# RMSNorm with GELU on one core: the first group scaled and stored row by row, its stores in 8 KB pieces

## The chip, the core and the metric

The kernel runs on one core of a Trainium2 chip. Times are device microseconds (us) of that core, taken from whole executions; the span in a profile is about 1.8 us shorter than the time of the same execution. Engines are named as in the profile: ACT (ScalarE), DVE (VectorE), POOL (GpSimd), PE (TensorE), SP (SyncE, which here only issues loads). "Faster" or "slower" needs a difference of 2%.

## The reference, cut

```python
# x: (8, 1024, 2048) float32, gamma: (2048,)
rms = np.sqrt(np.mean(x ** 2, axis=-1, keepdims=True) + eps)
out = gamma * x / rms
return 0.5 * out * (1 + np.tanh(np.sqrt(2 / np.pi) * (out + 0.044715 * out ** 3)))
```

Each of the 8192 rows is read once and written once: 67.1 MB in and 67.1 MB out.

## The kernel before

The rows are cut into 16 groups. A group has 128 partitions with 4 consecutive rows each, so a partition's share is 32 KB of contiguous memory, and a group is 4 MB. There are six slots in on-chip memory. A group is loaded whole, squared and summed row by row on ACT, scaled by gamma on DVE in place, put through GELU on ACT in place (with 1/rms as the scale of the activation), and stored whole from ACT's queue. The slot is then free for the load of group g + 6.

```python
P, ROWS, SLOTS = 128, 4, 6
x3 = ... .rearrange("(g p r) d -> g p r d", p=P, r=R)      # cut
slot = [sbuf.tile([P, R, D], FP32, name=f"slot{i}") for i in range(SLOTS)]

store_pieces = {G - 1: [(0, 2), (2, 2)]}
scale_pieces = {G - 1: [(0, 1), (1, 1), (2, 1), (3, 1)]}

def load(g):
    nc.sync.dma_start(out=slot[g % SLOTS], in_=x3[g])

def squares(g):                       # 4 ACT activations with accum_out (cut)
def scale(g):
    for r, n in scale_pieces.get(g, [(0, R)]):
        ...                           # one DVE multiply by gamma of n rows (cut)

def gelu_store(g):
    for r, n in store_pieces.get(g, [(0, R)]):
        for q in range(r, r + n):
            row = slot[g % SLOTS][:, q, :]
            nc.scalar.activation(out=row, in_=row, func=ACT.Gelu_apprx_tanh,
                                 scale=rstd[:, g, q : q + 1])
        nc.scalar.dma_start(out=o3[g, :, r : r + n, :],
                            in_=slot[g % SLOTS][:, r : r + n, :])

for g in range(SLOTS):
    load(g)
...                                   # gamma, constants (cut)
for g in range(G + 1):
    if g < G:
        squares(g); inverse_rms(g); scale(g)
    if g:
        gelu_store(g - 1)
        if g - 1 + SLOTS < G:
            load(g - 1 + SLOTS)
```

## Time and profile before

| | before |
|---|---|
| time, median of 3 | 317.33 us (317.2 to 317.46) |
| ACT busy | 79% |
| DVE busy | 44% |
| moved by DMA | 134.25 MB at 424 GB/s |
| a 32 KB packet on one DMA engine | 1.213 us (432 GB/s over 16 engines) |
| first store issued | 38.6 us |
| load 6, the first that needs a free slot, issued | 64.0 us |

The page of the kernel before, of a profiled execution that took 318.66 us and is not one of the three timed. The "DMA" row gives the busy share of the 16 DMA engines in 40 equal slices of the span, in tenths; the row under it is what they moved. The line with percent signs is the chain of waits that ended last, as shares of the span. The last two lines are the transfers, with KB each and the median us from issue to landing.

```profile
span 316.9 us, 473 instructions
...
PE 7.2 (2%) x8; PEld 2.5 (1%) x8; DVE 139.4 (44%) x21; ACT 251.1 (79%) x194; POOL 32.3 (10%) x101
...
DMA  8999999999999999999999999999999999999995
GB/s 328 414 451 426 434 393 459 401 459 402 459 405 455 426 434 431 430 434 426 438 426 455 410 455 418 443 426 430 434 430 435 422 459 405 459 414 447 422 420 230
DMA packets 4787, 134.25 MB, mean 424 GB/s; under 512 B 544, under 2 KB 560, under 8 KB 560
...
DMA 56%; ACT 33%; issue 5%; ACTq 1%; SPq 0%
...
slot<-in_x_dram SPq DMA_DIRECT2D x16, 4096.0 KB, 37.1
out_dram<-slot ACTq DMA_DIRECT2D x15, 4096.0 KB, 38.6
```

The DMA row is full from the second slice to the next to last.

The trace also holds every DMA packet with its start, duration, size and queue. "Packet time" is the sum of the durations of all load and store packets, divided by 16: what an average DMA engine had to do. "Stretch" is the time from the first packet's start to the last packet's end. For this profile the stretch is 313.83 us and the packet time 312.23 us: the engines worked almost without a break. At 1.213 us per 32 KB packet the bytes alone need about 310.5 us. By the profile's own zero of time the first packet starts at 1.7 us and the last ends at 315.6 us; the prediction below has both some 0.35 us later, and it rounds the rate to 433 GB/s and the time of the bytes to 309.7 us.

ACT has waits of its own. From the list of waits (total us, times, longest us):

```profile
...
ACT junk L65 <- DMA slot<-in_x_dram: 43.7, 11, 10.3
```

From the timeline of ACT (start us, us, instruction, and in brackets the idle time before it with its releaser), the place that the change works on:

```profile
...
30.93 7.67 ACT L101 ACTIVATE slot<-slot,rstd 128x2048 f32<-128x2048 f32 x4
...
38.62 0.36 ACTq L105 DMA_DIRECT2D out_dram<-slot  x1
```

From the timeline of SP's queue, the first load that has to wait for a free slot (with the one after it, merged in one line):

```profile
...
63.96 19.69 SPq L61 DMA_DIRECT2D slot<-in_x_dram  x2
```

And the end, from the timeline of ACT:

```profile
...
276.24 1.88 ACT L65 ACTIVATE junk<-slot 128x2048 f32<-128x2048 f32 x1 [3.66 <-DMA slot<-in_x_dram]
...
300.64 0.34 ACTq L105 DMA_DIRECT2D out_dram<-slot  x1
```

The GELU of group 0 begins at 30.9 us, because ACT squares group 1 first, and the whole group's store is issued at 38.6 us. The load at 63.96 us is load 6, which had to wait until that store had landed. At the end, the last load has landed by 276.2 us and the last store, 2.1 MB or some 5 us of DMA work, is issued at 300.6 us. By the packet records the DMA engines work until 315.6 us: even at the end ACT is ahead of them.

### The profile page before, as it was taken

The numbers are of one execution on the slowest core, as the hardware profiler recorded it, in microseconds if no ns is written. First come the engines' busy times: TensorE is split into PE (matmuls) and PEld (weight loads), VectorE is DVE, ScalarE is ACT, GpSimd is POOL, SyncE is SP. The second block draws the span as 40 slices with busy tenths as digits, with TensorE's granted clock in tenths as the row PEclk, the third lists the DMA queues.
The fourth block names the chain that finished last, engine by engine and source line by source line (L and its number), as shares of the span: only waits on it lengthen the run. The fifth ranks groups of instructions, "written<-read, shape, count | busy, mean of one in ns | idle before, by whom it ended". The sixth has DMA issues, their size and how long they took to land.

```text
span 316.9 us, 473 instructions
## 1 busy us (share of the span) xinstructions
PE 7.2 (2%) x8; PEld 2.5 (1%) x8; DVE 139.4 (44%) x21; ACT 251.1 (79%) x194; POOL 32.3 (10%) x101
## 2 busy tenths in 40 slices
PE   0900000000000000000000000000000000000000
PEld 0300000000000000000000000000000000000000
DVE  0038909090919191732808246091550905582000
ACT  1379999999999997959689595995959859599800
POOL 0020102020202020202002020020200102001000
DMA  8999999999999999999999999999999999999995
GB/s 328 414 451 426 434 393 459 401 459 402 459 405 455 426 434 431 430 434 426 438 426 455 410 455 418 443 426 430 434 430 435 422 459 405 459 414 447 422 420 230
DMA packets 4787, 134.25 MB, mean 424 GB/s; under 512 B 544, under 2 KB 560, under 8 KB 560
## 3 DMA queue, kind: packets, MB, share of 16 engines
q1 hardware_dynamic: 2304, 67.11, 49.5%
q10 hardware_dynamic: 2480, 67.12, 49.1%
q14 instruction: 3, 0.02, 0.0%
HBM read 67.12 MB, written 67.11 MB: 424 GB/s over the span
## 4 chain that ended last, share of the span: by engine, by line
DMA 56%; ACT 33%; issue 5%; ACTq 1%; SPq 0%
DMA slot<-in_x_dram 30%; DMA out_dram<-slot 26%; ACT slot L101 19%; ACT junk L65 14%; ACTq L105 1%; SPq L61 0%; ACTq L101 0%; ACTq L65 0%
## 5 line engine op out<-in xcount | busy, mean ns | idle before, releaser
L75 DVE TENSOR_TENSOR slot<-slot,gamma_ps 128x8192 f32<-128x8192 f32 (+1 forms) x19 | 139.2, 7340 | 147.0 <-ACT junk L65 147.0
L65 ACT ACTIVATE junk<-slot 128x2048 f32<-128x2048 f32 x64 | 120.4, 1881 | 47.3 <-DMA slot<-in_x_dram 43.7
L101 ACT ACTIVATE slot<-slot,rstd 128x2048 f32<-128x2048 f32 x64 | 122.8, 1989 | 0.9 <-ACT slot L101 0.9
L85 POOL TENSOR_SCALAR ms<-ssq 128x4 f32<-128x4 f32 x16 | 3.1, 194 | 247.5 <-ACT junk L65 247.5
L89 POOL TENSOR_TENSOR y<-ms,power 128x4 f32<-128x4 f32 x16 | 16.1, 1009 | 1.3
L65 ACT ACTIVATION_READ_ACCUMULATOR junk<-slot 128x1 f32 x64 | 12.0, 188 | 0.0
L121 PE MATMUL gamma_ps<-gamma_row,ones 1*128 1x512 f32 x8 | 7.2, 1072 | 8.4 <-DMA gamma_row<-in_gamma_dram 8.4
L95 POOL TENSOR_TENSOR rstd<-z,y 128x4 f32<-128x4 f32 x16 | 3.2, 201 | 1.3
L91 POOL TENSOR_TENSOR z<-z,ms 128x4 f32<-128x4 f32 x16 | 3.2, 201 | 1.3
L90 POOL TENSOR_TENSOR z<-y 128x4 f32<-128x4 f32 x16 | 3.2, 199 | 1.3
L92 POOL TENSOR_SCALAR z<-z 128x4 f32<-128x4 f32 x16 | 3.1, 194 | 1.4
L121 PEld LDWEIGHTS gamma_ps<-gamma_row,ones 1*128 1x128 f32 x8 | 2.5, 325 | 11.5 <-issue 11.5
L119 ACT ACT_TABLE_LOAD x1 | 1.3, 1283 | 1.3 <-PEq L153 1.3
L117 DVE MEMSET warm<- 1x1 f32 x1 | 0.1, 59 | 0.8 <-PEq L153 0.8
L119 ACT ACTIVATE warm<-warm 1x1 f32<-1x1 f32 x1 | 0.2, 202 | 0.0
L118 DVE MEMSET ones<- 1x128 f32 x1 | 0.2, 165 | 0.0
L116 POOL MEMSET power<- 128x4 f32 x1 | 0.1, 102 | 0.3 <-POOLq L153 0.3
L153 POOL MEMSET const-float32-0.0<- 128x1 f32 x1 | 0.1, 99 | 0.2 <-issue 0.2
L153 POOL MEMSET const-bfloat16-1.0<- 128x1 bf16 x1 | 0.1, 102 | 0.0
L153 POOL MEMSET const-uint8-127<- 128x1 uint8 x1 | 0.1, 102 | 0.0
L153 POOL MEMSET const-float32-1.0<- 128x1 f32 x1 | 0.1, 99 | 0.0
## 6 DMA issues: line engine op xcount, KB each, us to landing
slot<-in_x_dram SPq DMA_DIRECT2D x16, 4096.0 KB, 37.1
out_dram<-slot ACTq DMA_DIRECT2D x15, 4096.0 KB, 38.6
out_dram<-slot ACTq DMA_DIRECT2D x2, 2048.0 KB, 15.0
gamma_row<-in_gamma_dram ACTq DMA_DIRECT2D x1, 8.0 KB, 7.5
```

The source lines that it names most:

```text
L65: nc.scalar.activation(out=junk, in_=slot[g % SLOTS][:, r, :], func=ACT.Square, accum_out=ssq[:, g, r : r + 1],)
L75: nc.vector.tensor_tensor(out=rows, in0=rows, in1=gamma_ps.unsqueeze(1).to_broadcast([P, n, D]), op=ALU.mult,)
L85: v.tensor_scalar(out=ms, in0=ssq[:, g, :], scalar1=1.0 / D, scalar2=eps_f, op0=ALU.mult, op1=ALU.add,)
L89: v.tensor_tensor(out=y, in0=ms, in1=power, op=ALU.pow)
L90: v.tensor_tensor(out=z, in0=y, in1=y, op=ALU.mult)
L91: v.tensor_tensor(out=z, in0=z, in1=ms, op=ALU.mult)
L92: v.tensor_scalar(out=z, in0=z, scalar1=-0.5, scalar2=1.5, op0=ALU.mult, op1=ALU.add)
L95: v.tensor_tensor(out=rstd[:, g, :], in0=z, in1=y, op=ALU.mult)
L101: nc.scalar.activation(out=row, in_=row, func=ACT.Gelu_apprx_tanh, scale=rstd[:, g, q : q + 1],)
L105: nc.scalar.dma_start(out=o3[g, :, r : r + n, :], in_=slot[g % SLOTS][:, r : r + n, :])
L119: nc.scalar.activation(out=warm, in_=warm, func=ACT.Gelu_apprx_tanh)
L121: nc.tensor.matmul(out=gamma_ps[:, k : k + 512], lhsT=ones, rhs=gamma_row[:, k // GW : (k + 512) // GW, 0:GW], start=True, stop=True,)
```

## The change

The intent is to send the first output off earlier: once row 0 of group 0 has its GELU, it goes out, while rows 1 to 3 are still in work. DVE's multiply is cut by rows too.

```diff
-    store_pieces = {G - 1: [(0, 2), (2, 2)]}
-    scale_pieces = {G - 1: [(0, 1), (1, 1), (2, 1), (3, 1)]}
+    single = [(0, 1), (1, 1), (2, 1), (3, 1)]
+    store_pieces = {0: single, G - 1: [(0, 2), (2, 2)]}
+    scale_pieces = {0: single, G - 1: single}
```

A row of a partition is 8 KB, and the next partition's row is 32 KB further on, so a row's store consists of 128 pieces of 8 KB where the whole group's store had 128 pieces of 32 KB.

## The prediction

> **What bounds it now.** The DMA engines. The page shows 134.25 MB at a mean of 424 GB/s. In the transfer records the 16 engines hold packets without a gap from 2.1 us to 315.9 us of the 316.9 us span. A 32 KB packet takes 1.213 us on one engine (433 GB/s over 16), load or store; at that pace the bytes need 309.7 us. The rest the change hardly touches: 2.1 us before the first packet, 1.0 us after the last, 0.7 us of slow first load packets, 0.6 us of slow packets near 41 us, where the first store arrives, and small dips.
>
> ACT (79%) isn't the limit: the waits show 43.7 us for loads, from 119 us on about 3.7 us a group. DVE (44%) waits for ACT.
>
> **How the rings share.** From the first store on, each engine's records alternate load packet, store packet, both 32 KB. The Trainium skill, "DMA: Bandwidth & Descriptors", section "Queues, rings and completion order", says engines round-robin between queue rows by packet; this trace agrees, with one 32 KB descriptor acting as the packet. The first store was issued at 38.6 us and landed at 63.9 us; only then was load 6 issued.
>
> **What changes.**
> - DVE: one scale of 8.69 us becomes four of about 2.2 us, starting after the first square (15.2 us, not 21.3). ACT gains nothing: it squares group 1 until 31.0 us anyway.
> - ACT: 3 more store issues of 0.34 us, and broken GELU pipelining (7.67 us for four in a row, 3.90 for two): about +1.5 us where ACT is 96% busy. The first store goes out at about 33.2 us.
> - DMA: same bytes; 384 more data packets and 48 more completion writes (4787 become about 5219). From 16 KB at 0.611 us and 32 KB at 1.213 us I estimate 0.31 us for 8 KB, +0.2 us in all.
> - Sharing: an 8 KB store packet alternates with a 32 KB load packet, so the first stores get a fifth of the bandwidth while loads 4 and 5 are queued. An estimate, stepping the rings with these durations: load 5 lands near 68 us, not 82; load 6 is issued at 71 to 76 us, not 64. The load ring is then empty some 4 us, but the store ring holds rows of group 0 and all of group 1, so no engine idles. Later loads land earlier, stores queue longer; the last load lands some 8 us before its 276 us.
>
> **How much is critical.** Almost none. A change of order helps only where DMA idles, and only the fixed ends do. Ending ACT earlier (last store issued at 300.6 us, last packet at 315.9) only lengthens the store backlog.
>
> Prediction: 317.6 us, 316.9 to 318.6 in 8 of 10. Chances: faster by 2% 0.01, within 2% 0.97, slower 0.02.
>
> **What would show the steps.** Packets near 5219; 8 KB packets near 0.31 us; first stores issued at 33 to 41 us; load 6 issued past 70 us; no slice of low DMA share between 40 and 80 us; store landings longer and load landings shorter (medians now 38.6 and 37.1 us).
>
> **What would make it wrong.** Dearer 8 KB packets (each 0.1 us more is 3.2 us in all); sharing by bytes, not packets (load 6 before 64 us, time still the same); both rings empty near 70 us; or the dip at the first store vanishing, or repeating per piece (0.6 us each).

## More of the kernel before

GB/s swings from slice to slice, but over longer stretches, in the view by windows, the rate is even. The columns of that view are the stretch, its length, the busy time (and count) of PE, PE's weight loads, DVE, ACT and POOL, the clock, the DMA share, and GB/s:

```profile
...
40.00:80.00 40.00, 0.00 (x0) 0.00 (x0) 18.01 (x3) 38.89 (x33) 4.49 (x14) 1.00 1.01 431
80.00:120.00 40.00, 0.00 (x0) 0.00 (x0) 25.19 (x3) 38.08 (x28) 5.49 (x17) 1.00 1.01 433
120.00:280.00 160.00, 0.00 (x0) 0.00 (x0) 71.47 (x10) 128.42 (x99) 15.97 (x48) 1.00 1.00 432
```

## The result, and the profile after

The changed kernel took 318.3 us (median of 4, 318.18 to 318.51), the kernel before 317.39 us in its runs (317.2 to 318.41). The ratio is 1.0023 with a 95% interval of 1.0001 to 1.0045: the same, by the 2% rule. (A ratio is the mean time of one kernel's fast runs over that of the other's fast runs of the same rounds, so it is not quite the ratio of the medians quoted.) The time lies in the predicted range of 316.9 to 318.6 us.

The same lines of the page after the change:

```profile
span 316.6 us, 478 instructions
...
PE 7.2 (2%) x8; PEld 2.5 (1%) x8; DVE 139.6 (44%) x24; ACT 251.3 (79%) x194; POOL 32.1 (10%) x101
...
DMA  8999999999999999999999999999999999999996
GB/s 328 414 447 426 423 409 432 454 439 402 398 447 410 455 414 448 431 431 435 426 443 418 451 414 451 410 460 414 447 436 422 443 418 447 418 451 414 447 408 279
DMA packets 5219, 134.25 MB, mean 424 GB/s; under 512 B 592, under 2 KB 608, under 8 KB 608
...
ACT 37%; DMA 31%; another core or an unknown queue 18%; issue 6%; ACTq 1%; SPq 0%
...
slot<-in_x_dram SPq DMA_DIRECT2D x16, 4096.0 KB, 27.2
out_dram<-slot ACTq DMA_DIRECT2D x14, 4096.0 KB, 44.3
out_dram<-slot ACTq DMA_DIRECT2D x4, 1024.0 KB, 28.9
```

The DMA row has not changed, nor have the bytes or the mean rate. There are 5219 packets instead of 4787. Loads land faster (27.2 us instead of 37.1), stores of whole groups land later (44.3 us instead of 38.6). The chain that ended last is now given to ACT for 37% and no longer mainly to DMA; experiment e7 below shows how little that share means here.

The view by windows after the change, columns as before:

```profile
...
40.00:80.00 40.00, 0.00 (x0) 0.00 (x0) 17.38 (x2) 38.47 (x32) 3.98 (x12) 1.00 1.01 428
80.00:120.00 40.00, 0.00 (x0) 0.00 (x0) 24.18 (x3) 38.98 (x30) 5.97 (x18) 1.00 1.00 424
120.00:280.00 160.00, 0.00 (x0) 0.00 (x0) 77.94 (x12) 133.86 (x106) 16.22 (x50) 1.00 1.00 433
```

The stretch from 80 to 120 us has lost: 424 GB/s instead of 433, which is 0.8 us of 40; some slow packets near 85 us are the reason, and they are taken up after the experiments. From 120 us on the two kernels run alike.

From the list of waits of ACT:

```profile
...
ACT junk L66 <- DMA slot<-in_x_dram: 36.5, 9, 10.4
```

From the timeline, DVE and ACT at the first group:

```profile
...
15.77 8.88 DVE L76 TENSOR_TENSOR slot<-slot,gamma_ps 128x2048 f32<-128x2048 f32 x4 [14.77 <-PE gamma_ps L122]
...
31.03 1.99 ACT L102 ACTIVATE slot<-slot,rstd 128x2048 f32<-128x2048 f32 x1
...
33.05 0.36 ACTq L106 DMA_DIRECT2D out_dram<-slot  x1
...
35.49 0.34 ACTq L106 DMA_DIRECT2D out_dram<-slot  x1
...
37.90 0.34 ACTq L106 DMA_DIRECT2D out_dram<-slot  x1
...
40.32 0.34 ACTq L106 DMA_DIRECT2D out_dram<-slot  x1
```

From the timeline of SP's queue, loads 6 and 7:

```profile
...
71.87 17.75 SPq L62 DMA_DIRECT2D slot<-in_x_dram  x2
```

From the timeline of ACT, the end:

```profile
...
271.41 1.88 ACT L66 ACTIVATE junk<-slot 128x2048 f32<-128x2048 f32 x1 [3.67 <-DMA slot<-in_x_dram]
...
295.79 0.34 ACTq L106 DMA_DIRECT2D out_dram<-slot  x1
```

The four stores are issued at 33.05, 35.49, 37.90 and 40.32 us, the first 5.6 us earlier than the one store of before and the last 1.7 us later. But load 6 is issued at 71.87 us, 7.9 us *later* than before. The packet records show why. Between 45 and 65 us loads moved at about 350 GB/s and stores at 81 GB/s, 4.3 to 1: the rates fit an engine that takes a load packet of 32 KB and a store packet of 8 KB in turn. In the kernel before they moved about equally (222 and 211 GB/s), 32 KB against 32 KB. Load 5, still in the queue then, landed at 68.4 us instead of 82.0, and group 0's last row landed at 71.82 us, where the whole group had landed at 63.88 us. The last load landed 4.8 us earlier than before (ACT starts on it at 271.41 instead of 276.24 us), the last store was issued 4.9 us earlier (295.79 instead of 300.64 us), and the span is nevertheless 316.6 us against 316.9.

The Trainium skill, "DMA: Bandwidth & Descriptors", section "Queues, rings and completion order", says that an engine goes round-robin over the queue rows that have work, packet by packet. This trace agrees, and it shows that the unit is the single piece (32 KB or 8 KB), not an equal number of bytes.

### The profile page after: what moved, and what is told of

The parts are those of the page before. It is cut to its first block, busy times and chain, and to the rows that moved or that the text cites. A ratio compares the mean times of both kernels' runs of the same rounds, so it can differ in the third digit from the quotient of the medians.

```text
span 316.6 us, 478 instructions
## 1 busy us (share of the span) xinstructions
PE 7.2 (2%) x8; PEld 2.5 (1%) x8; DVE 139.6 (44%) x24; ACT 251.3 (79%) x194; POOL 32.1 (10%) x101
## 2 busy tenths in 40 slices
DMA packets 5219, 134.25 MB, mean 424 GB/s; under 512 B 592, under 2 KB 608, under 8 KB 608
## 4 chain that ended last, share of the span: by engine, by line
ACT 37%; DMA 31%; another core or an unknown queue 18%; issue 6%; ACTq 1%; SPq 0%
ACT slot L102 21%; ACT junk L66 16%; DMA out_dram<-slot 16%; DMA slot<-in_x_dram 15%; ACTq L106 1%; SPq L62 0%; ACTq L102 0%; ACTq L66 0%
## 6 DMA issues: line engine op xcount, KB each, us to landing
slot<-in_x_dram SPq DMA_DIRECT2D x16, 4096.0 KB, 27.2
out_dram<-slot ACTq DMA_DIRECT2D x14, 4096.0 KB, 44.3
```

## The experiments

Theory A: the 16 DMA engines never stand idle between the first packet and the last, so the time is the bytes over the rate; sending the same bytes in another order gains nothing, and what remains is the small cost of more and smaller packets. The rivals: a gain and a loss cancel (C); the moment of the first store counts (F); ACT is the limit (G); the early stage has slack, so nothing done there shows (H).

All experiments were timed in 3 or 5 rounds beside the kernel before on the same chip. The kernel before scatters more than its first three runs told: from 317.14 to 319.3 us over all these rounds.

### e1: the changed kernel again

No edit.

> The changed kernel itself, timed anew beside the kernel before. Theory A (the DMA engines are full all the time, so a new order of the same bytes changes nothing; only 384 smaller packets are added): 0 to +0.6 us. Rival B (a real loss of about 1 us, as the first ratio of 1.0023 suggests, from the four small stores): +0.7 us or more, and again in every round.

Measured: 318.28 us (317.83 to 318.47), before 317.8 us (317.17 to 319.3), ratio 1.0005 (0.9985 to 1.0026). No difference can be told from the times. The lowest times differ by 0.66 us. The packet time is 313.07 us, against 312.84 us in the first profile of the changed kernel and 312.23 us in that of before; this is taken up at e9.

### e2: scale by rows, store whole

```diff
-    store_pieces = {0: single, G - 1: [(0, 2), (2, 2)]}
+    store_pieces = {G - 1: [(0, 2), (2, 2)]}
```

> Only the scale of group 0 row by row, stored whole. Theory A: within 0.4 us of before, and the trace much as before: first store issued at 38.6 us, load 6 issued near 64 us, because ACT squares group 1 until 31 us anyway. Rival C (the change holds a gain from the early scale and a loss from the small stores, which cancel): faster than before by 0.7 us or more.

Measured: 317.35 us, ratio 0.998 (0.996 to 1.0), packet time 312.13 us. The first store was issued at 38.7 us and load 6 at 63.1 us, much as before. By the ratio the run is 0.6 us faster than before, which lies between what theory A allows (0.4 us) and what rival C asks (0.7 us). The kernel before itself took 317.33 us in e9, so I count it as no gain: ACT is not waiting for the early scale.

### e3: store by rows, scale whole

```diff
-    scale_pieces = {0: single, G - 1: single}
+    scale_pieces = {G - 1: single}
```

> Only the stores of group 0 row by row, scaled whole (DVE ends that scale at 30.0 us, before ACT is free at 31.0 us). Theory A: the same as the changed kernel within 0.4 us: first store near 33 us, load 6 issued near 72 us, 8 KB packets at 0.309 us. Rival C: slower than before by 1.5 us or more.

Measured: 317.98 us, ratio 0.9998 (0.9976 to 1.0019), packet time 313.02 us. Rival C needs a loss of 1.5 us here, and the interval ends at 0.6 us: rival C falls. The interval of e2 alone would still allow a gain of up to 1.3 us; its packet time, that of before within 0.1 us, shows none.

### e5: the first store 10 us later

```diff
-            if g:
-                gelu_store(g - 1)
-                if g - 1 + SLOTS < G:
-                    load(g - 1 + SLOTS)
+            if g < 2:
+                continue
+            for d in range(0 if g == 2 else g - 1, g):
+                gelu_store(d)
+                if d + SLOTS < G:
+                    load(d + SLOTS)
```

> The kernel before, but the first group's GELU and store come after the squares of group 2: the first store is issued near 48.5 us instead of 38.6 us. Theory A (only idle DMA time costs; the six loads in the queue keep the engines full until 48 packets x 1.213 us, that is to about 61 us): same as before within 0.6 us. Rival F (the time of the first store counts, so that the change should have gained by 5.5 us of earlier issue): about +10 us.

Measured: 318.56 us, ratio 1.0018 (0.9989 to 1.0047); the first store was issued at 48.3 us. Ten microseconds of delay cost nothing that the rounds resolve. Rival F falls. (Its packet time, 313.30 us, is higher than before; see e9.)

### e6: the first store after the loads have run out

The same edit with 4 in place of 2.

> The same with the first store after the squares of group 4: issued near 67.7 us, its first packet near 69.3 us, while the six loads end near 61 us. Theory A: the DMA engines stand idle some 8.3 us, and the time grows by just that: about 326 us (ratio 1.026). Rival F: +29 us. Rival G (ACT sets the time, and it does the same work in another order, with no idle stretch of its own before its later waits for loads): same as before.

Measured: 325.92 us, ratio 1.0253 (1.0225 to 1.0281), as theory A had it. Its page has a hole in the DMA row:

```profile
span 324.5 us, 477 instructions
...
DMA  8999999469999999999999999999999999999997
```

The view by windows (columns as above) at the hole:

```profile
...
60.00:70.00 10.00, 0.00 (x0) 0.00 (x0) 8.69 (x1) 9.51 (x7) 2.00 (x6) 1.00 0.13 56
```

The DMA share is 0.13 from 60 to 70 us, where ACT is busy for 9.51 of the 10 us. The stretch is 8.4 us longer than the packet time, and the time grew by 8.0 us (0.0253 x 318 us). So the same delay is free as long as the six loads keep the engines full, and costs one for one after that. This also speaks against rival G: ACT did the same work.

### e7: a third less work on ACT

```diff
-                out=junk,
-                in_=slot[g % SLOTS][:, r, :],
+                out=junk[:, 0:512],
+                in_=slot[g % SLOTS][:, r, 0:512],
```

> The kernel before with each square over 512 of the 2048 columns only (a wrong result on purpose): some 80 to 90 us of ACT work gone, ACT from 79% to about 52%. Theory A: same as before within 1 us. Rival G (ACT is the limit, as the chain that ended last gives it 37% of the changed kernel): faster by 5% or more.

Measured (the result is wrong): 317.45 us, ratio 0.9979 (0.9954 to 1.0005). From its page:

```profile
span 315.9 us, 470 instructions
...
PE 7.2 (2%) x8; PEld 2.5 (1%) x8; DVE 139.4 (44%) x21; ACT 169.0 (54%) x194; POOL 32.3 (10%) x101
...
DMA  8999999999999999999999999999999999999996
```

ACT is busy 169.0 us instead of 251.1, and the time has not moved. Rival G falls. The 33% that the chain gives ACT before, and the 37% after, are the way by which waits pass from one transfer to the next; they are not time that a faster ACT would give back.

### e8: half of the first store left out

```diff
+            if g == 0 and r >= 2:
+                continue
             nc.scalar.dma_start(
```

> The changed kernel with rows 2 and 3 of group 0 not stored (a wrong result on purpose): 2.10 MB less at the same early place that the change works on. Theory A: 2.10 MB at 433 GB/s, 4.84 us less than the changed kernel: near 313.3 us. Rival H (the early stage has slack, so nothing done there shows): less than 1 us.

Measured (wrong; two rows of group 0 are not written): 312.57 us, ratio 0.9828 (0.98 to 0.9855). That is 5.7 us less than the changed kernel's 318.28 us. The bytes alone account for 4.85 us (2.10 MB at 432 GB/s); the packet time fell by 5.6 us, from 312.84 to 307.26 us, so the rest are fewer slow packets. At the very place where a new order gains nothing, fewer bytes gain in full. Rival H falls.

### e4: the same treatment for groups 0 to 14

```diff
-    store_pieces = {0: single, G - 1: [(0, 2), (2, 2)]}
-    scale_pieces = {0: single, G - 1: single}
+    store_pieces = {**{g: single for g in range(G - 1)}, G - 1: [(0, 2), (2, 2)]}
+    scale_pieces = {g: single for g in range(G)}
```

> Groups 0 to 14 all scaled and stored row by row. Theory A: only the packet cost grows: four 8 KB packets take 4 x 0.309 us for the 1.213 us of one of 32 KB, 0.023 us more, times 8 packets an engine, times 15 groups: +2.8 us, near 320.2 us, with the DMA still full although ACT gets 15 times 1.5 us more work. Rival D (what a first group loses or gains by order repeats with each group): 15 times the effect seen for one group, that is anything from -10 to +14 us, and not the packet sum.

Measured: 342.53 us, ratio 1.0768 (1.0741 to 1.0794). Both expectations missed; I had forecast 320.2 us. Packet time is 319.33 us, 7.1 us more than before, and the stretch is 18.5 us longer than it: the DMA engines stood idle. The view by windows, columns as above:

```profile
...
42.00:116.00 74.00, 0.00 (x0) 0.00 (x0) 27.87 (x13) 49.29 (x39) 5.96 (x18) 1.00 1.00 418
116.00:270.00 154.00, 0.00 (x0) 0.00 (x0) 69.82 (x32) 122.74 (x94) 15.91 (x48) 1.00 1.01 422
270.00:341.00 71.00, 0.00 (x0) 0.00 (x0) 26.64 (x12) 56.79 (x41) 5.97 (x18) 1.00 0.71 296
```

From the list of waits, ACT in front of a GELU:

```profile
...
ACT slot L102 <- DMA slot<-in_x_dram: 28.2, 8, 7.6
```

And a piece of ACT's timeline:

```profile
...
245.74 2.00 ACT L102 ACTIVATE slot<-slot,rstd 128x2048 f32<-128x2048 f32 x1 [0.42 <-ACT slot L102]
251.23 0.34 ACTq L106 DMA_DIRECT2D out_dram<-slot  x1
251.62 2.00 ACT L102 ACTIVATE slot<-slot,rstd 128x2048 f32<-128x2048 f32 x1 [3.88 <-DMA slot<-in_x_dram]
```

In the first of these windows ACT is busy for 49.29 of 74 us, where in the kernel before it was busy for 71.90 us in the same stretch. The GELU of a third row ends at 247.7 us, but its store is issued only at 251.23 us, and the next GELU stands behind it; the profile names a load as the releaser. The trace's records of issues and landings show what this is: all transfers, loads and stores, share eight completion semaphores (counters that tell of a landing), and in none of the runs is a transfer issued before the one that used its semaphore last has landed. The store at 251.23 us has the semaphore of load 14, which landed at 251.16 us. With five transfers per group instead of two, a semaphore comes round after less than two groups, and ACT, which issues the stores, is held up by a transfer in flight: nine stores are held, 36.8 us in all, eight by a load and one, for 11.7 us, by an earlier store. (The changed kernel has a harmless form of this: its loads 4 and 5 were issued at 8.38 and 22.95 us, just after the gamma load and load 1 had landed, and not at 2.67 and 3.15 us as before.) ACT falls behind, and when the loads are over (from about 270 us), it can't deliver stores as fast as the DMA engines could send them: DMA share 0.71 over 71 us.

Is it that, or the small packets, or the precedence that 32 KB load packets have over 8 KB store packets? Three more runs.

### e7b: 8 KB packets for everything, one transfer per group

```diff
-    slot = [sbuf.tile([P, R, D], FP32, name=f"slot{i}") for i in range(SLOTS)]
+    wide = [sbuf.tile([P, R, D + 16], FP32, name=f"slot{i}") for i in range(SLOTS)]
+    slot = [w[:, :, 0:D] for w in wide]
```

> The kernel before on slots whose rows are 64 bytes apart, so that every load and every store moves in 8 KB packets, still one transfer per group. Asked: what made the all-rows kernel 24 us slower and not 2.8 us. Theory P (it was the small packets as such): 8 KB packets on both sides, so at least as slow as that kernel, over 340 us. Theory A's packet sum: 0.023 us x 8 x 32 transfers = +5.9 us, near 323.7 us, with the rings sharing half and half again (load 6 issued near 64 us) and the DMA full to the end.

Measured: 320.92 us, ratio 1.0087 (1.0063 to 1.0111). Small packets as such cost 2.8 us for *all* 32 transfers, half of what I had estimated. (The recorded durations of 8 KB packets, 0.309 us, overlap a little: here their sum, 317.30 us per engine, is above the stretch of 315.64 us, which can't be. So the packet time of kernels with many 8 KB packets is somewhat too high, by at least 1.66 us for these 1024 packets per engine, and by at least 0.05 us for the 32 packets per engine of group 0 alone.)

### e7c: 8 KB packets for everything, stored row by row

Both edits, e7b's and e4's.

> The same wide slots, and groups 0 to 14 scaled and stored row by row, so that 8 KB load packets alternate with 8 KB store packets and loads have no precedence, while ACT still issues four stores per group, each of which has to wait until an older transfer with the same one of eight completion semaphores has landed. Theory S (ACT is held up at these issues): as slow as the all-rows kernel, about 340 us. Theory Q (loads took four fifths of the bandwidth, so ACT's backlog of loaded groups was worked off at the end with idle DMA engines): near the one-transfer kernel with 8 KB packets, 323 to 327 us.

Measured: 344.52 us, ratio 1.0827 (1.0797 to 1.0857). The packets are of equal size, so loads have no precedence, and the loss is as in e4: theory Q falls. From the list of waits, ACT's wait for loads in front of a GELU:

```profile
...
ACT slot L103 <- DMA slot<-in_x_dram: 39.6, 8, 13.8
```

The stretch is 20 us longer than the packet time. What differs from e7b is the number of transfers (and the scale cut by rows, which e2 showed to be harmless for one group). What differs too are the gaps of some 0.4 us that every further store leaves on ACT. Theory S fits, with the wait of 39.6 us and the records of the semaphores as its evidence. I found no way to keep the row stores and be rid of these waits alone, so that the waits cause the loss is read from the trace, and not shown by a run without them.

### e8h: all groups stored in two halves

```diff
-    store_pieces = {G - 1: [(0, 2), (2, 2)]}
+    store_pieces = {g: [(0, 2), (2, 2)] for g in range(G)}
```

> The kernel before with every group stored as two transfers of 16 KB pieces. Theory S (the all-rows kernel lost its time because the compiled program gives eight completion semaphores to all transfers in turn: with five transfers a group, the third row's store must wait for a load that was issued less than two groups ago and has not landed): with three transfers a group a semaphore comes round after 2.7 groups, such waits end before they are reached, ACT shows no wait for a load ahead of a GELU, and only the packets cost: (2 x 0.611 - 1.213) us x 8 x 15 = +1.1 us, near 319 us. Rival (more and smaller stores lose time by their number, whatever the waits): a third of the all-rows kernel's loss, +8 us, as there is one more transfer a group in place of three.

Measured: 325.41 us (324.21 to 326.97), ratio 1.0253 (1.0211 to 1.0295). Theory S was wrong about the time, and about the waits too. The list of waits has none in front of a GELU any more, but ACT's timeline has them in another place:

```profile
...
101.63 3.90 ACT L101 ACTIVATE slot<-slot,rstd 128x2048 f32<-128x2048 f32 x2 [0.42 <-ACT slot L101]
110.72 0.34 ACTq L105 DMA_DIRECT2D out_dram<-slot  x1
111.11 1.88 ACT L65 ACTIVATE junk<-slot 128x2048 f32<-128x2048 f32 x1 [5.58 <-DMA slot<-in_x_dram]
```

The GELU ends at 105.5 us, and its store is issued only at 110.72 us, 0.08 us after the landing of load 7, which had the same semaphore. The squares behind it are those of group 6, which had landed at 88.5 us; the list puts the wait down to them. Seven stores are held in this way, 26.8 us in all. So the run does not separate the number of stores from the waits, as it was meant to, and the rival's +8 us, though it came true, is not confirmed against theory S.

An estimate from the lists of waits says why e4 ends with idle DMA engines and this run does not. Before, ACT waits 43.7 us for loads, 10.3 of them for the first: 33 us of slack. In e4 the held stores (36.8 us) and the gaps that the extra pieces leave (22.2 us where there were 3.0) add 56 us, far more than the slack; here it is 26.8 us and 7 us, about as much. No run isolates this. From its page:

```profile
span 323.7 us, 517 instructions
...
GB/s 325 445 401 449 421 421 429 445 389 467 407 439 437 419 407 448 397 405 431 409 429 411 403 425 447 401 433 428 413 431 423 427 425 435 427 429 435 431 429 111
```

The last slice is nearly empty, at 111 GB/s (230 in the kernel before). By the packet records the packet time is 317.07 us, 5.0 us above that of e9 below, and in the last 3 us only one of the 16 engines was still at work, which adds 3.2 us of idle time. Of the 5.0 us, 1.1 us are the price of 16 KB packets; the rest are single packets that took up to 1.4 us longer than the usual 1.213 or 0.611 us. What makes these packets slow is open; when they come is taken up at the end of the next section.

### e9: the kernel before against itself

No edit.

> The kernel before against itself, for the scatter and for a second look at its DMA records. Theory A in its last form (storing group 0 by rows costs 0.6 us of packet time, 312.84 to 313.07 us per engine in three profiles against 312.23 in the one of before, and the rest of the differences is how far the last of the 16 engines lags behind the others, which varies from run to run): ratio within 0.997 to 1.003, lowest time 317.1 to 317.3 us, summed packet time 312.1 to 312.4 us per engine whatever the time of the profiled run. If the packet time comes out at 312.8 us or more, the 0.6 us is scatter too.

Measured: 317.33 us (317.23 to 317.49), ratio 0.9993 (0.9982 to 1.0005), packet time 312.08 us, as expected. The sums of all runs, in us (that of e7b is too high, as said there):

| run | median | ratio | packet time | stretch less packet time |
|---|---|---|---|---|
| before | 317.33 | | 312.23 | 1.60 |
| e9 before again | 317.33 | 0.9993 | 312.08 | 0.46 |
| e2 scale by rows only | 317.35 | 0.998 | 312.13 | 0.37 |
| after | 318.3 | 1.0023 | 312.84 | 0.69 |
| e1 after again | 318.28 | 1.0005 | 313.07 | 0.55 |
| e3 store by rows only | 317.98 | 0.9998 | 313.02 | 0.03 |
| e5 first store later | 318.56 | 1.0018 | 313.30 | 0.35 |
| e6 first store too late | 325.92 | 1.0253 | 312.99 | 8.41 |
| e7 less ACT work | 317.45 | 0.9979 | 312.29 | 0.58 |
| e8 half of first store | 312.57 | 0.9828 | 307.26 | 0.55 |
| e4 all by rows | 342.53 | 1.0768 | 319.33 | 18.46 |
| e7b 8 KB, whole groups | 320.92 | 1.0087 | 317.30 | -1.66 |
| e7c all by rows, 8 KB | 344.52 | 1.0827 | 319.42 | 19.99 |
| e8h all by halves | 325.41 | 1.0253 | 317.07 | 3.66 |

Before, e9 and e2 have 312.08 to 312.23 us of packet time, the three profiles with row stores of group 0 have 312.84 to 313.07: a cost of about 0.8 us. It is not a cost of row stores as such: e5, which stores whole groups but moves the first store, has 313.30 us. The timed rounds alone do not resolve it. They are blurred by the kernel before: in its first profile, a run of 318.66 us, two of the 16 engines were still at work 1.5 us before the last packet's end; in that of e9, a run about a microsecond shorter, nine were 1.0 us before it. The last engine's lag is idle time for the others, 1.60 us against 0.46.

No version came out that beats both kernels. With the engines full from 1.7 us on, little but fewer bytes would help, and the reference needs them all.

## Why the prediction was right

- **The limit.** DMA bound, as predicted. e7 (82 us of ACT work gone, no gain), e8 (half of one store gone, full gain) and e6 (8.4 us of idle DMA, 8.0 us of loss) show it.
- **No gain from the earlier first store.** As predicted. Its 5.6 us are worth nothing, since the loads fill the engines; e5's 10 us later cost nothing either.
- **The early scale.** As predicted, worthless (e2), since ACT squares group 1 until 31.0 us. It began at 15.77 us instead of the 15.2 us that I gave, as DVE had to wait for gamma.
- **Work on ACT.** About +1.5 us predicted; the next group's store went out at 56.41 instead of 54.74 us, +1.7 us, without effect.
- **Sharing by pieces.** As predicted: 4.3 to 1 where a fifth was forecast for the stores, load 5 at 68.4 us (68), load 6 issued at 71.87 us (71 to 76), 5219 packets (5219), 8 KB packets at 0.309 us (0.31), no slice of low DMA share.
- **The empty load ring.** By a ring the prediction means the packets of one queue that wait at a DMA engine. "Some 4 us" was too short: by the packet records no load packet was under way for 8.2 us, from 67.8 to 76.0 us, and 4.2 us of this passed between the issue of load 6 and its first packet. No engine idled, as argued: the stores alone held them. But slow packets followed, which the prediction did not foresee here.
- **The last load.** Forecast 8 us earlier, measured 4.8 us.
- **The term that was mis-sized.** "+0.2 us in all" for smaller packets. The changed kernel is dearer by about 0.8 us in packet time. The 8 KB packets account for 0.1 to 0.2 us of it. The rest, some 0.6 us, are packets, mostly of loads, that took 1.3 to 2.9 us instead of 1.213: the kernel before has one such episode after the start, 0.59 us near 41 us, when the first store joins; the changed kernel has them spread from 35 to 45 us (0.44 us together), near 75 us (0.13 us), when load 6 joins, and at 85 us (0.69 us). I had named a repetition of this dip as a way to be wrong. It is small enough for the range to hold.

What stays open is what makes those packets slow. They come near moments when a stream of transfers joins or changes, also in e5 (0.89, 0.28 and 0.73 us). The profiles of all runs sort them further. In before, e9, e2, e7 and e8 the load ring is never empty for over 2.5 us, and packets over a tenth longer than usual cost 0.6 to 0.9 us after the first 10 us. In after, e1, e3, e5 and e6 it runs empty once, for 5.5 to 22.7 us, and they cost 1.2 to 1.9 us, of which 0.8 to 1.3 us come from then until 12.5 us after the loads resume. In e8h it runs empty nine times, for about 4 to 8 us, and 3.7 of 4.4 us come at such times, which are half of its span. So the extra packet time goes with an empty load ring and not with the size of the pieces: e8 stores by rows without it, e5 has it without rows. Only e7c, with 8 KB packets, does not fit, and no run isolates a cause.

## What to carry to other kernels

Before moving work earlier, ask whether the resource that it feeds is idle at that time: here the first store could come 10 us later or 5 us earlier for nothing, and only when the DMA engines had run dry did each microsecond count. Two queues on the same DMA engines shared them by pieces here, so cutting the pieces of one queue by four hands four fifths of the bandwidth to the other. And cutting transfers up is cheap in packets but not in transfers: done to every group, it made the issuing engine wait for completion semaphores, and the kernel took 7.7% longer (how much of this is due to the waits no run isolates). A list of waits can hide such a hold: look at the time between the end of the work and the issue of its store.

## What the Trainium skill lacked or had wrong

- "DMA: Bandwidth & Descriptors", section "Queues, rings and completion order": it says that a packet typically holds 9 to 17 descriptors. Here each piece of 32 KB, 16 KB or 8 KB is a record of its own, and the engines change queues after each one (350 against 81 GB/s for 32 KB against 8 KB pieces).
- The same page, section "Where 436 GB/s comes from": it says that for transfers between HBM and on-chip memory the HBM side, about 358 GB/s, binds, though its own measured loads of a single core are faster. This one-core kernel held 432 GB/s from 120 to 280 us, half loads and half stores, which is next to the 435 GB/s that the section gives for the fabric.
- The same page, section "Measured" under "Bandwidth", asks for at least 1 MiB per transfer and gives 341 GB/s for a load of 1 MB on another issue path. In a full queue, stores of 1 MB ran in 8 KB packets of 0.309 us, that is 424 GB/s over 16 engines; with such stores for all groups but the last (e4), idle DMA engines cost more (18.5 us) than the longer packet time (7.1 us).
- The same page, section "Latency and other measured facts", has two DMA engines that are usually slower and, as a best guess, ties this to the software-issued path. Both queues here are of the hardware-issued kind, and some engines still end later than the others (the records do not tell which): 1.60 us and 0.46 us of stretch were left beside the packet time in two profiles of the same kernel.
- I found on no page the slow packets that come near the start or change of a stream of transfers (0.59 us at the first store before, 1.26 us in all after the change), most of the added ones after the load queue had run empty for 8.2 us.
